# Rooms for the weight ring in two pools, a branch moved ahead of the last second products, and an inversion cut into five steps

## The chip, the cores and the metric

One core of a Trainium2 chip runs the kernel. The metric is the device time of one execution in microseconds, the median of several runs. Engines are called TensorE (PE in the rows), VectorE (DVE), ScalarE (ACT), GpSimd (POOL) and SyncE (SP); a "q" behind an engine's name means its queue of instructions (its sequencer).

## The reference, cut to what matters

256 tokens of width 1024 go through two layers, all in float32. The first is a hybrid of windowed attention and a gated delta rule; the second has two kinds of attention heads and then 32 experts, of which each token uses four, and a gated embedding at the end.

```python
def gated_deltanet(q, k, v, g, beta):            # chunks of 64 tokens
    m = where(strict, (k*beta) @ k.T * decay, 0)
    sol = triangular_solve(m + eye, concat([v*beta, k*beta*exp(G)]))   # unit lower triangle
    ...
def moe(u, ...):                                 # 256 tokens, top 4 of 32 experts
    hh = xs @ w_gu[e] + b_gu[e]                  # 1024 -> 2048 (first products)
    glu, lin = split(hh); glu = min(glu, 7); lin = clip(lin, -7, 7)
    act = glu * sigmoid(1.702*glu) * (lin + 1)
    return act @ w_dn[e] + b_dn[e]               # 1024 -> 1024 (second products)
def second_block(x, ...):
    ...
    h = h + moe(rmsnorm(h, g_moe), ...)
    u = rmsnorm(h, g_ple)
    h = h + sigmoid(u @ w_ple_gate) * (p @ w_ple_proj)
    return rmsnorm(h, g_final)
```

## The kernel before, in words

**Projections.** Weights of the dense layers come as pieces of 128 x 2048 float32 (1 MiB): `load` (L104) takes a room of a ring of rooms and issues the DMA on SP's queue, `piece` (L120) splits it with `split` (L314): ScalarE casts the high part, VectorE subtracts it from the source and leaves the low part. Each product is then three matmuls: activations' high part by the weights' high and low part, and activations' low part by the weights' high part. `proj_T_g` (L198) and `proj_tok_g` are generators that yield after a few products; `proj_rows` (L137) makes 256 rows by 1024 columns, 512 columns at a time, and hands each 128x512 result to a function that evacuates it.

**First stage.** `together` (L228) writes the program order: in each round every live generator (attention and delta rule, per half of the heads) makes one step, and then the fill (the projections) runs until its own count has reached 2.5 us. `gdn_half` (L597) is the delta rule for four heads. It writes its triangles to DRAM, reads them back as 64 blocks (`X`), inverts them on VectorE in `inverse` (L577: 15 columns, two operations for each), then pauses once, writes the blocks to `diag`, reads them back (L660), and transposes them on TensorE. The zeros of `diag` come from a tile that VectorE clears (L573). Within an engine's queue the tile framework's scheduler may order instructions otherwise than the program does, unless they are pinned with `keep_in_program_order`.

**The ring of weights.** SBUF pools are stacked. `st` lies low and has 3 rooms called raw, 2 whi and 2 wlo. After the first stage the pools `wa` (8 tiles of 4 KB per partition) and `wb` hold the second attention. When they close, the pool `raw2` (L1116) of 8 rooms (4 raw, 2 whi, 2 wlo; 64 KB per partition) takes their place: it covers `wa` (32 KB) and the first 32 KB of `wb`. The ring then has 15 rooms (`raws`, L1118). `ahead` (L1148) fills the first 11 of them, in the order of `raws` by program, before the experts start; `refill`, called after each product group in `run` (L1484), takes the room that was read. All weights of the 32 experts (384 MiB) go through it, raw, in 1 MiB loads.

**The experts.** `run` works through 17 units: pairs of experts, one expert of up to 128 rows, and the last expert, 31, alone. Step i does the first products of unit i, then the second products of unit i-1 (L1370 in both cases), `gated` (L1453: ScalarE and VectorE scale the result by the gates) and later `combine` (L1462: a matmul scatters it to tokens and VectorE adds to `hres`). Matmuls of `run` are pinned in program order.

**The tail.** After `run` the four loads of the gate weights (`gate_w`) go into the raw rooms of `raw2` and the first of them is split. `further` (L1618) is a branch on a register that counts tokens over the units' limits; with these inputs it is not taken. Then the last unit is combined, normed and transposed for both halves of the tokens (L1716 to L1729), with the splits of the other three gate pieces in between, the final projection runs on TensorE (`proj_rows` with four wide pieces) and `ev` (L1734) evacuates it: sigmoid, times the embedding, add, square for the final norm, and the output.

## Time and profile before

| what | value |
|---|---|
| median of 3 runs | 1570.43 us (1569.9 to 1571.59) |
| the profiled execution | 1570.8 us, its span 1568.9 us |
| busy share of the span | TensorE 91%, VectorE 39%, ScalarE 27%, GpSimd 2% |
| mean rate of the DMA over the span | 311 GB/s |
| operations on GpSimd | 39 |

The page cuts the span into 40 slices of 39.2 us. Up to slice 14 the core computes dense layers, from slice 15 to 38 the experts' weights stream in, and the last slice and a half hold the final projection. A timeline row gives the start, the busy time, the engine and line, the operation, how often it stands there in a row, and in brackets how long its engine was idle before it and who released it. Times that a row gives for a merged group run from its first start to its last end.

### The profile page before, as it was taken

To read this page: it belongs to the slowest core of one execution; us is meant where nothing else is said; L and a number is where in the kernel's file an instruction comes from. 1 tells how busy PE (TensorE), PEld (TensorE's weight loads), DVE (VectorE), ACT (ScalarE), POOL (GpSimd) and SP (SyncE) were. 2 spreads that over 40 slices of the span, in tenths; PEclk is the share of its full clock that TensorE was granted. 3 is DMA by queue.
4 is the path that set the end of the run, shared out by engine and by line. 5 is a ranking of instruction groups with operands and counts; after the bars stand their busy time and mean duration, and the time that the engine had idled before them with its cause. 6 is when DMAs were issued, how large, how long until landed. Compare 5 with 4: busy or idle time off the path is not lost. (4 is left out here: it accounts for less than half of the span.)

```text
span 1568.9 us, 20018 instructions
## 1 busy us (share of the span) xinstructions
PE 1431.5 (91%) x7922; PEld 883.2 (56%) x7922; DVE 619.3 (39%) x1215; ACT 418.6 (27%) x638; POOL 27.1 (2%) x39
## 2 busy tenths in 40 slices
PE   6999998999889989989888998999988889989887
PEld 6889898999689864424334334434433324424335
DVE  6868865456656662112123122112312202302236
ACT  5543644443447621101001001101100101101124
POOL 0000100000000000000000000000000000000000
PEclk9999999999899989999999999999999999999998
DMA  7544244355344189999999999999999999999981
GB/s 241 163 150 150 90 141 130 108 188 173 127 132 141 55 345 421 421 421 421 421 421 419 421 421 421 421 421 420 421 421 421 421 420 420 421 422 421 421 350 67
DMA packets 108541, 487.58 MB, mean 311 GB/s; under 512 B 14766, under 2 KB 23356, under 8 KB 59292
## 3 DMA queue, kind: packets, MB, share of 16 engines
q1 hardware_dynamic: 108300, 485.87, 78.2%
q8 instruction: 64, 1.05, 0.3%
q0 software_dynamic: 144, 0.39, 0.1%
q14 instruction: 33, 0.27, 0.0%
HBM read 483.48 MB, written 2.75 MB: 310 GB/s over the span
## 5 line engine op out<-in xcount | busy, mean ns | idle before, releaser
L1370 PE MATMUL ph<-raw,xs 128*64 128x512 f32 (+1 forms) x936 | 241.7, 594 | 5.7 <-DMA raw<-in_w_gu_dram 5.6
L1370 PE MATMUL ph<-wlo,xs 128*64 128x512 f32 (+1 forms) x552 | 192.3, 594 | 4.8 <-DMA wlo<-in_w_gu_dram 4.8
L1370 PE MATMUL ph<-whi,xs 128*64 128x512 f32 (+1 forms) x560 | 194.6, 594 | 2.0 <-DMA whi<-in_w_gu_dram 2.0
L316 DVE TENSOR_TENSOR wlo<-raw,whi 128x2048 fp32r<-128x2048 f32 (+4 forms) x73 | 158.0, 2165 | 91.8 <-ACT whi L315 91.7
L212 PE MATMUL pm<-w,wlo 128*128 128x256 f32 x640 | 182.5, 286 | 6.6 <-DVE wlo L316 6.6
L210 PE MATMUL pm<-w,whi 128*128 128x256 f32 x640 | 185.1, 290 | 3.3 <-ACT whi L315 3.3
L1557 DVE COPY hs<-ph 128x512 f32<-128x512 f32 x34 | 23.5, 692 | 406.4 <-PE ph L1370 406.4
L211 PE MATMUL pm<-w,whi 128*128 128x256 f32 x640 | 183.0, 286 | 0.0
L315 ACT CAST whi<-raw 128x2048 fp32r<-128x2048 f32 (+4 forms) x73 | 131.9, 1806 | 141.3 <-PE pm L211 88.1
L1370 PE MATMUL pm<-raw,act 128*64 128x512 f32 (+1 forms) x520 | 137.9, 597 | 29.0 <-DMA raw<-in_w_dn_dram 29.0
L1370 PEld LDWEIGHTS ph<-raw,xs 128*64 128x64 f32 (+1 forms) x936 | 78.1, 138 | 144.9 <-issue 130.8
L1557 ACT COPY hs<-ph 128x512 f32<-128x512 f32 x34 | 19.9, 586 | 412.6 <-PE ph L1370 412.6
L212 PEld LDWEIGHTS pm<-w,wlo 128*128 128x128 f32 x640 | 124.0, 194 | 7.5 <-DVE wlo L316 7.5
L210 PEld LDWEIGHTS pm<-w,whi 128*128 128x128 f32 x640 | 124.3, 194 | 4.1 <-ACT whi L315 3.9
L211 PEld LDWEIGHTS pm<-w,whi 128*128 128x128 f32 x640 | 124.5, 194 | 0.3
L1460 DVE SCALAR_TENSOR_TENSOR yl<-pm,gs,yh 128x512 fp32r<-128x512 f32 x32 | 24.0, 750 | 251.1 <-ACT yh L1459 250.4
L1370 PEld LDWEIGHTS ph<-wlo,xs 128*64 128x64 f32 (+1 forms) x552 | 61.6, 139 | 83.1 <-issue 72.8
L1370 PEld LDWEIGHTS ph<-whi,xs 128*64 128x64 f32 (+1 forms) x560 | 60.8, 138 | 81.5 <-issue 73.8
L1370 PEld LDWEIGHTS pm<-raw,act 128*64 128x64 f32 (+1 forms) x520 | 42.5, 137 | 113.6 <-issue 62.3
L1370 PE MATMUL pm<-wlo,act 128*64 128x512 f32 (+1 forms) x256 | 87.8, 597 | 11.8 <-DMA wlo<-in_w_dn_dram 11.5
L1459 ACT ACTIVATE yh<-pm,gs 128x512 fp32r<-128x512 f32 x32 | 22.0, 687 | 266.6 <-PE pm L1370 265.1
L1370 PE MATMUL pm<-whi,act 128*64 128x512 f32 (+1 forms) x248 | 82.5, 597 | 10.4 <-DMA whi<-in_w_dn_dram 10.4
(399 smaller groups left out, 1921.4 us busy)
## 6 DMA issues: line engine op xcount, KB each, us to landing
raw<-in_w_gu_dram SPq DMA_DIRECT2D x117, 1024.0 KB, 19.8
whi<-in_w_gu_dram SPq DMA_DIRECT2D x70, 1024.0 KB, 19.8
wlo<-in_w_gu_dram SPq DMA_DIRECT2D x69, 1024.0 KB, 19.8
raw<-in_w_dn_dram SPq DMA_DIRECT2D x65, 1024.0 KB, 19.8
raw<-in_w_in_dram SPq DMA_DIRECT2D x46, 1024.0 KB, 5.6
wlo<-in_w_dn_dram SPq DMA_DIRECT2D x32, 1024.0 KB, 20.0
whi<-in_w_dn_dram SPq DMA_DIRECT2D x31, 1024.0 KB, 19.8
raw<-in_w_branch_a_dram SPq DMA_DIRECT2D x4, 1024.0 KB
```

The costliest lines, as they stand in the source:

```text
L210: T.matmul(o, hi[:, k, ns], xh[:, k0 + k], start=first, stop=False)
L211: T.matmul(o, hi[:, k, ns], xl[:, k0 + k], start=False, stop=False)
L212: T.matmul(o, lo[:, k, ns], xh[:, k0 + k], start=False, stop=last)
L315: A.copy(hi, src)
L316: (by or V).tensor_tensor(lo, src, hi.bitcast(F32), ALU.subtract)
L1370: return tc.keep_in_program_order(T.matmul(*x_, **y_))
L1459: A.activation(yh[:, ns], yp[n_], AF.Copy, scale=b["gs"])
L1460: V.scalar_tensor_tensor(yl[:, ns], yp[n_], b["gs"], yh[:, ns].bitcast(F32), ALU.mult, ALU.subtract)
L1557: (V.tensor_copy if j // 2 else A.copy)(b["hs"][j // 2][:, j % 2 * 512:j % 2 * 512 + 512], hp[j])
```

## The change

1. *First products.* The load of the second half of x goes ahead of the two small vector loads on SP. The tile of zeros is cleared by GpSimd. `proj_T_g`, for a piece that was loaded ahead, does all products with the high part of the first piece first, and then those with the low part.
2. *Inversion.* `inverse` becomes a generator that pauses after every third column: five pauses, the last of which stands where the one pause behind it stood.
3. *Ring.* `raw2` keeps its 4 raw rooms; its whi and wlo rooms move to a pool of their own, `raw3`. The ring's order becomes raw2's raw, raw3's whi and wlo, then the rooms of `st`. The loads of `ahead` are pinned in program order on SP. Three tiles that nothing uses (640, 320 and 192 bytes per partition) shift the places of pools.
4. *Tail.* Every step of `run` ends with its outstanding combines. `further`, and behind it the four loads of the gate weights, is called in the last step ahead of the second products of the last unit. The gate pieces 1, 2 and 3 are all split behind the first half of the tokens, 2 and 3 with the subtraction on GpSimd. The last 128x512 group of the final projection is made and evacuated in two halves of 256 columns.

```diff
     SY.dma_start(ctab[0], a["const"][:, :cuts[1]])
+    SY.dma_start(hres[:, 1], xsrc[:, 1])
...
+    cst.tile([P, 160], F32, name="gap0")
...
-        SY.dma_start(raw[:, :kc * n].rearrange("p (k n) -> p k n", k=kc), src.rearrange(rows, p=P))
+        d_ = SY.dma_start(raw[:, :kc * n].rearrange("p (k n) -> p k n", k=kc), src.rearrange(rows, p=P))
+        if pin:
+            tc.keep_in_program_order(d_)
         return raw
...
             for nh in range(2):
+                for h in (0, 1) if halves and t and nh else (None,):
+                    ps = pp.tile([P, 512], F32, name=name)
+                    cs = slice(0, 512)
+                    if h is not None:
+                        ps, cs = ps[:, :256], slice(h * 256, h * 256 + 256)
...
+                    evac(t, nh, ps) if h is None else evac(t, nh, ps, h)
...
             hi, lo = piece(w[k0 * P:(k0 + 4) * P], 4, 512, raw and raw[k0 // 4])
+            if raw and k0 == 0:
+                for lo_ in range(2):
+                    for b in range(2):
+                        for j in range(2):
+                            ns = slice((2 * b + j) * P, (2 * b + j + 1) * P)
+                            o = ps[b][:, j * 256:(j + 1) * 256]
+                            for k in range(4):
+                                if lo_:
+                                    T.matmul(o, lo[:, k, ns], xh[:, k], start=False, stop=False)
+                                else:
+                                    T.matmul(o, hi[:, k, ns], xh[:, k], start=k == j == 0, stop=False)
+                                    T.matmul(o, hi[:, k, ns], xl[:, k], start=False, stop=False)
+                        yield 1.0 + lo_
+                continue
...
         SY.dma_start(v0[8 * i:8 * i + 8], a[n].rearrange("o (c p) -> (o c) p", p=P))
-    SY.dma_start(hres[:, 1], xsrc[:, 1])
...
-        V.memset(zero, 0.0)
+        G.memset(zero, 0.0)
...
                 V.tensor_tensor(o, o, tmp[:, :n, :m], ALU.subtract)
+                if j % 3 == 2:
+                    yield 0.0
...
-            inverse(X, Y)
-            yield 0.0
+            yield from inverse(X, Y)
...
     raw2 = ctx.enter_context(tc.tile_pool(name="raw2", bufs=1))
-    raws[:] = [(raw2, "raw", RAW2), (st, "raw", RAW), (raw2, "whi", 2), (raw2, "wlo", 2), (st, "whi", HL), (st, "wlo", HL)]
-    parts.append((raw2, 2))
+    raw3 = ctx.enter_context(tc.tile_pool(name="raw3", bufs=1))
+    raws[:] = [(raw2, "raw", RAW2), (raw3, "whi", 2), (raw3, "wlo", 2), (st, "raw", RAW), (st, "whi", HL), (st, "wlo", HL)]
+    parts.append((raw3, 2))
...
-        return [(load(src, kc, m, pool, rows), kc, m) for src, kc, m, rows in (next(order) for _ in range(n))]
+        return [(load(src, kc, m, pool, rows, True), kc, m) for src, kc, m, rows in (next(order) for _ in range(n))]
...
+                if i == n and ahead_of_last:
+                    ahead_of_last()
                 if i:
                     b = units[i - 1]
...
-                if i != n - 1:
-                    flush()
+                flush()
                 after(i)
...
             every = raws[:]
-            raws[:] = [(st, "raw", RAW)]
+            raws[:] = [(st, "whi", HL)]
...
             raws[:] = every
+            gate_w.extend(rows_piece(a["w_ple_gate_2"][0], i, big) for i in range(4))
...
-        last = run(units, order, ready, {-1: first, 2: [load_biases], ...})
+        last = run(units, order, ready, {-1: first, 2: [load_biases], ...}, None, further)
...
         count[1] = 0
-        gate_w = [rows_piece(a["w_ple_gate_2"][0], i, big) for i in range(4)]
         gate_w[0] = piece(None, 4, 512, gate_w[0])
-
-        further()
-        count[1] = 1
...
-            for i in ((1, 2), (3,))[t]:
-                gate_w[i] = piece(None, 4, 512, gate_w[i])
+            if t == 0:
+                gate_w[1:] = [piece(None, 4, 512, g_, by) for g_, by in zip(gate_w[1:], (V, G, G))]
...
-        proj_rows(ph, None, None, xh, xl, ev, gate_w, 4, "ph")
+        proj_rows(ph, None, None, xh, xl, ev, gate_w, 4, "ph", True)
```

Left out are the argument lists, the two other unused tiles, and `ev` and `total`, which take the half `h` and add three sums of squares in place of two.

## Rows read from the trace of the kernel before

**Rows 1.** The page: GB/s moved in each of 40 equal slices of 39.2 us.
```profile
GB/s 241 163 150 150 90 141 130 108 188 173 127 132 141 55 345 421 421 421 421 421 421 419 421 421 421 421 421 420 421 421 421 421 420 420 421 422 421 421 350 67
```

**Rows 2.** Windows: length, busy us of PE, PEld, DVE, ACT, POOL, clock, DMA, GB/s.
```profile
0.00:440.00 440.00, 407.92 (x2903) 381.61 (x2904) 290.08 (x488) 211.22 (x287) 18.16 (x24) 0.98 0.46 148
...
558.00:1522.00 964.00, 879.62 (x4167) 378.15 (x4167) 224.80 (x555) 113.66 (x187) 3.02 (x5) 0.99 1.01 420
```

**Rows 3.** Timeline of TensorE, 0 to 20 us: start, busy, operation, idle before, releaser.
```profile
13.82 0.58 PE L210 MATMUL pm<-w,whi 128*128 128x256 f32 x1 [2.38 <-ACT whi L315]
...
16.45 0.58 PE L212 MATMUL pm<-w,wlo 128*128 128x256 f32 x1 [1.41 <-DVE wlo L316]
```

**Rows 4.** Timeline of TensorE around 126 and 247 us.
```profile
125.94 0.38 PE L212 MATMUL pm<-w,wlo 128*128 128x256 f32 x1 [2.51 <-DVE wlo L316]
...
247.16 1.94 PE L304 MATMUL pm<-C,w 128*128 128x128 f32 x8 [4.79 <-DMA w<-diag]
```

**Rows 5.** Windows at the first inversion and behind the gap after it.
```profile
111.20:123.50 12.30, 12.23 (x102) 12.03 (x101) 11.81 (x44) 5.51 (x5) 0.00 (x0) 1.00 0.53 171
128.00:132.00 4.00, 4.00 (x25) 4.00 (x25) 2.36 (x8) 0.59 (x1) 0.00 (x0) 0.66 1.07 358
```

**Rows 6.** Lines L736 and L795: duration ns min/median/max, first and last start, form.
```profile
L736 ACT ACTIVATE w<-pm,gdnw x4: 678/680/682, 190.2 to 311.3; 128x512 f32<-128x512 f32 x4
...
L795 ACT ACTIVATE w<-pm x8: 582/597/606, 270.5 to 346.2; 128x512 f32<-128x512 f32 x8
```

**Rows 7.** Timeline of SP, 470 to 600 us: DMA issues.
```profile
531.13 27.90 SPq L116 DMA_DIRECT2D raw<-in_w_gu_dram  x7
...
585.51 10.63 SPq L116 DMA_DIRECT2D raw<-in_w_gu_dram  x7
```

**Rows 8.** One window ahead of the stream.
```profile
522.00:557.00 35.00, 32.38 (x181) 26.80 (x180) 19.83 (x31) 15.21 (x24) 2.20 (x4) 0.95 0.16 61
```

**Rows 9.** Timelines of TensorE and VectorE between 514 and 600 us.
```profile
521.35 0.66 PE L304 MATMUL pm<-C,w 128*128 128x128 f32 x4 [0.94 <-ACT w L386]
...
556.29 0.68 DVE L316 TENSOR_TENSOR w<-w,w 128x512 fp32r<-128x512 f32 x1
...
581.83 10.94 PE L1370 MATMUL ph<-raw,xs 128*64 128x512 f32 x49
```

**Rows 10.** Timeline of TensorE at 1471 us and in the tail.
```profile
1471.19 3.65 PE L1370 MATMUL pm<-raw,act 128*64 128x512 f32 x14 [1.32 <-DMA raw<-in_w_dn_dram]
...
1521.64 1.94 PE L1370 MATMUL pm<-wlo,act 128*64 128x512 f32 x8 [0.28 <-SPq L1623]
1523.51 2.24 PE L1370 MATMUL pm<-hs,ohT 128*128 128x512 f32 x8
1529.82 0.47 PE L1370 MATMUL pm<-yh,ohT 128*128 128x512 f32 x1 [4.07 <-DVEq L1623]
...
1537.91 0.50 PE L159 MATMUL ph<-wlo,raw 128*128 128x512 f32 x1 [1.19 <-DVE wlo L316]
```

**Rows 11.** Line L1623, the branch: sequencers' durations ns, first and last start.
```profile
L1623 SPq EVENT_SEMAPHORE  x9: 17/17/17, 1518.4 to 1530.0; - x9
...
L1623 PEldq COMPARE_BRANCH  x1: 3822/3822/3822, 1525.0 to 1525.0; - x1
L1623 ACTq COMPARE_BRANCH  x1: 50/50/50, 1525.7 to 1525.7; - x1
```

**Rows 12.** Timelines of SP and VectorE in the tail.
```profile
1509.37 21.14 SPq L116 DMA_DIRECT2D raw<-in_w_ple_gate_dram  x4
...
1516.18 1.57 DVE L1460 SCALAR_TENSOR_TENSOR hs<-pm,gs,hs 128x512 fp32r<-128x512 f32 x2 [11.75 <-ACT hs L1459]
...
1527.33 2.29 DVE L316 TENSOR_TENSOR wlo<-raw,whi 128x2048 fp32r<-128x2048 f32 x1
```

**Rows 13.** Groups of GpSimd: xcount, busy us, mean ns, idle before.
```profile
L299 POOL TENSOR_TENSOR l_r<-rs_t,C 128x4 f32<-128x4 f32 x12 | 14.0, 1167 | 281.6 <-DVE rs_t L298 281.6
```

**Rows 14.** Timeline of ScalarE behind the last product.
```profile
1560.65 0.69 ACT L1738 ACTIVATE sw<-ph,n_r 128x512 f32<-128x512 f32 x1 [2.54 <-PE ph L160]
```

More of the change, by code (lines that the diff above doesn't have):

```diff
@@ L102, in slots, with load @@
         return sum(n_ for _, _, n_ in raws)
-    def load(src, kc, n, pool=None, rows="(k p) n -> p k n"):
+    def load(src, kc, n, pool=None, rows="(k p) n -> p k n", pin=False):
         if pool is None:
@@ L135, in rows_piece, with proj_rows @@
         return load(W[k0 * P:(k0 + 4) * P, nh * 512:(nh + 1) * 512], 4, 512, pool)
-    def proj_rows(pp, w, W, xh, xl, evac, raw=(), wide=2, name="pm"):
+    def proj_rows(pp, w, W, xh, xl, evac, raw=(), wide=2, name="pm", halves=False):
         pcs = []
@@ L398, in rope @@
         V.tensor_tensor(dst, t1, t2, ALU.add)
+    sm.tile([P, 80], F32, name="gap1", bufs=1)
     keep = Pool(ctx.enter_context(tc.tile_pool(name="keep", bufs=1)), w4=4)
@@ L407, in tile_net @@
         both = ctx.enter_context(tc.tile_pool(name="both", bufs=1))
+        both.tile([P, 48], F32, name="gap2")
         pm = c1.enter_context(tc.tile_pool(name="ps", bufs=4, space=bass.MemoryType.PSUM))
@@ L1482, in bias_of, with run @@
             return bi
-        def run(units, order, ready, more=None, room=None):
+        def run(units, order, ready, more=None, room=None, ahead_of_last=None):
             more = more or {}
@@ L1655, in further @@
             raws[:] = every
+            gate_w.extend(rows_piece(a["w_ple_gate_2"][0], i, big) for i in range(4))
         big = raw2, RAW2
-        pv, emb = [], []
+        pv, emb, gate_w = [], [], []
         def load_embed(nxt):
@@ L1687, in tile_net @@
         first = [lambda nxt, g=g: g() for g in (chosen, gates, changes, overflow)]
-        last = run(units, order, ready, {-1: first, 2: [load_biases], 3: [biases], 4: [blocks], 6: [load_embed], EMB - 1: [embed]})
+        last = run(units, order, ready, {-1: first, 2: [load_biases], 3: [biases], 4: [blocks], 6: [load_embed], EMB - 1: [embed]}, None, further)
         if "h3" in dbg:
@@ L1706, in tile_net, with total @@
         rr = []
-        def total(t):
+        def total(t, n=2):
             s1 = sm.tile([P, 1], F32, name="po_s1")
-            V.tensor_tensor(s1, ssq[:, t, 0:1], ssq[:, t, 1:2], ALU.add)
+            if n == 2:
+                V.tensor_tensor(s1, ssq[:, t, 0:1], ssq[:, t, 1:2], ALU.add)
+            else:
+                V.tensor_reduce(s1, ssq[:, t], AX.X, ALU.add)
             return rsqrt(s1, 1, 1.0 / D, EPS, "n_r")
@@ L1727, in tile_net, with ev @@
             rr.append(total(t))
-            for i in ((1, 2), (3,))[t]:
-                gate_w[i] = piece(None, 4, 512, gate_w[i])
-        ssq = sm.tile([P, 2, 2], F32, name="po_ss")
+            if t == 0:
+                gate_w[1:] = [piece(None, 4, 512, g_, by) for g_, by in zip(gate_w[1:], (V, G, G))]
+        ssq = sm.tile([P, 2, 3], F32, name="po_s3", bufs=1)
         og = {}
-        def ev(t, nh, ps):
-            ns = slice(nh * 512, nh * 512 + 512)
+        def ev(t, nh, ps, h=None):
+            cs = slice(0, 512) if h is None else slice(h * 256, h * 256 + 256)
+            ns = slice(nh * 512 + cs.start, nh * 512 + cs.stop)
             o = hres[:, t, ns]
-            sg = wk.tile([P, 512], F32, name="sw", bufs=4)
+            sg = wk.tile([P, 512], F32, name="sw", bufs=4)[:, cs]
             A.activation(sg, ps, AF.Sigmoid, scale=rr[t][:, :1])
@@ L1740, in ev @@
             V.tensor_tensor(o, o, sg, ALU.add)
-            A.activation(sg, o, AF.Square, accum_out=ssq[:, t, nh:nh + 1])
-            og[nh] = wk.tile([P, D], F32, name="hs", bufs=2)[:, :512]
-            V.tensor_tensor(og[nh], o, gf[:, ns], ALU.mult)
-            if nh == 0:
+            i = nh + (h or 0)
+            A.activation(sg, o, AF.Square, accum_out=ssq[:, t, i:i + 1])
+            if not h:
+                og[nh] = wk.tile([P, D], F32, name="hs", bufs=2)[:, :512]
+            V.tensor_tensor(og[nh][:, cs], o, gf[:, ns], ALU.mult)
+            if nh == 0 or h == 0:
                 return
-            r = total(t)
+            r = total(t, 2 + t)
             for b in range(2):
```

12 lines of the change are left out of this document (5 added, 7 removed).

## The prediction, on record before the change was run

> **What bounds the kernel now.** I read the slices of the page first, then the windows by stage, then the timelines around each place that the change touches. There are four stages. Up to about 440 us (the hybrid layer) TensorE is the bound: it is busy 407.9 of 440 us [rows 2], so whatever takes away idle time of TensorE there comes off the total. From 440 to 558 us the second attention block runs; the weight transfers have almost stopped (55 GB/s in slice 14, [rows 1]). From 558 to 1522 us the experts' weights stream in at 421 GB/s in nearly every slice [rows 1], while TensorE has idle time, 879.6 busy of 964 us [rows 2]: here the stream is the bound, one load of 1 MiB costs 1.0486 MB / 421 GB/s = 2.49 us, and only an earlier start (or a higher rate) helps. The last gap of TensorE that a weight load ends is at 1471 us [rows 10]; behind it the tail is a chain of TensorE, the branch and the last projection. So savings before the stream and in the tail add up, as long as the stream's rooms stay full.
>
> The trace is one execution of 1570.8 us (span 1568.9 and 1.9 around it); the median shown is 1570.43. I make the sum against the profiled run and take it off the median: the two differ by 0.4 us.
>
> **Part 1, the first products.** The first projection product waited 2.38 us for a cast that stands behind both halves of the first norm, and the first product with a low part waited 1.41 us for VectorE [rows 3]. The load of the second half of x goes ahead of the two small vector loads on SP's queue (these come later by one 512 KB load), the memset leaves VectorE, and the high products go first: 2 groups of 4 x 4 x 2 = 32 products at 0.12 us (102 products in 12.23 us, [rows 5]) are 3.8 us of cover for a low part that came 2.6 us after the first product (16.45 - 13.82). So the 1.41 goes wholly; of the 2.38 I take 0.6, since only one of its causes moves. Sum -2.0; bounds 0 (the small vectors, now later, hold the first evacuation) and -3.8. The memset of 128x512 goes to GpSimd, which has nothing else to do there; the two DMAs that read it come a little later and their readers only with the first inversion.
>
> **Part 2, the inversion in five steps.** No operation is added or taken away; the one pause behind it becomes five (after columns 2, 5, 8, 11 and 14, the last where the old one stood). So each chain gets four more rounds of at least 2.5 us of projection work by the planner's count, in program order. In the first inversion VectorE was busy 11.81 of 12.3 us [rows 5] and the low part of the next weight piece stood behind it: TensorE lost 2.51 us at 125.94 [rows 4], and its granted clock was 0.66 in the four microseconds from 128 (the lower of 1.2 and 2.4 GHz for part of it), another 0.34 x 4 = 1.4 us [rows 5]. With pieces between the steps the low part comes first: -3.9. In the second inversion VectorE had time, and the gap of 4.79 us at 247.16 waits for the trip through memory behind it [rows 4]; a loss of clock follows as behind the first. Four rounds give 10 us more cover; the chain itself becomes longer by the VectorE work of that fill (two splits of 2.29 us, [rows 12], and evacuations, some 5 to 7 us by that row). I take half of 4.79, -2.4, and count no clock. Of the -6.3 I give back 0.8 for waits that appear elsewhere: -5.5. Bounds: -10.1 (both gaps and twice the clock) and +4.8 (one more gap like the largest one). The later end is covered: the last evacuation of the two chains stands at 311.3, the last of the fill at 346.2 [rows 6], 35 us for 10 us of delay.
>
> **Part 3, the start of the ring.** Seven first loads go out from 531.13 [rows 7], but from 522 to 557 only 61 GB/s moved, 2.1 MB or two loads [rows 8]: the scheduler put rooms of `st` first, and the room `raw2` covers the attention pools `wa` and `wb` and so waits for the last work in `wb`, VectorE's 128x512 subtraction at 556.29 [rows 9]. `raw2` is now half as large and lies on `wa` alone, whose last reader is TensorE's transposes at 521.35 to 522.0 [rows 9]. Its four loads, pinned in order, can go at 522; then SP stands waiting at the first room of `raw3` until 556.9, and behind it are queued the three `st` rooms that went early before, which cost two loads of the old order. Nothing else waits on SP there: the next loads need rooms anyway. Four loads instead of two before 557 are 2 x 2.49 = 5.0 us. What is late next: there are 15 rooms, so 11 loads remain, 11 x 2.49 = 27.4 us from 557, done at 584.4 (the delay from issue to first byte stands at both ends and cancels), and the first room comes free for a refill at 585.51 [rows 7], which follows the first products at 581.83 [rows 9] that no load sets. The stream pauses for 1.1 us at this rate, for less where the loads come slower; I take 0.8: -4.2, bounds -2.7 (a pause of 2.3, when the second refill is late too) and -5.0.
>
> **Part 4, the tail.** Before: second products of the last unit to 1523.6, combine of the pair before it, branch, combine of the last at 1529.82 after 4.07 us of idle [rows 10]; SP stood inside the branch until its third gate load had landed at 1530.0, so the fourth left only then [rows 11, 12]. After: second products of the last pair end at about 1516.1 as now, when VectorE begins to gate them [rows 12]; its combine must wait for its gated rows (VectorE ends at 1517.75) and takes 2.24 us [rows 10], to 1520.0. Then the branch. Its compare-and-branch took 3.82 us on TensorE's sequencer, 0.05 us on ScalarE's [rows 11]. TensorE reached it 0.74 us before the end of the combine (1525.01 against 1525.75), so the last unit's products start between 1520.1 and 1523.2; I take the TensorE row, 1523.2. They take 7.4 us, 1.4 us more if the idle time lowers the clock as behind the gaps above: 1532.0, and gating 2 us: 1534.0, against 1529.8. Given back: between combine and projection VectorE did a split of 2.29 us [rows 12], which now follows; the continuous part of the projection started at 1537.9 to 1538.5 [rows 10] and now starts at about 1540, 1.7 later. The gate loads leave together when SP is out of the branch (1521.6, the landing of the last weight piece, [rows 10]), and cannot all be in before 1521.6 + 4 x 2.49 = 1531.6; the last is needed some 8 us into the projection. The last group is split into halves: the chain behind the last product has four operations of 0.69 us [rows 14], now of half width, -1.1 by estimate (0 to -1.4), and 48 products of 0.12 for 24 of 0.227 cost +0.3. Tail: +1.7 + 0.3 - 1.1 = +0.9, taken as +1.0; bounds -2 (short branch, full clock) and +6.
>
> Two of the gate splits go to GpSimd, whose only operation in the trace is a power of 128x4 in 1.17 us [rows 13]. Bounds for 128x2048: 2.29 us as on VectorE [rows 12], and 512 times 1.17, absurdly far; I take the first, since it is the same operation. With casts done by about 1534 and 1536.5 and the last low part needed at 1540 + 36 x 0.227 = 1548.2, two operations one after the other cost nothing up to T = 7 us each. The Trainium skill speaks against the move: "GPSIMD Engine Reference", section 3.1, gives 4497 ns for this operation against 2293 ns on VectorE, and calls VectorE the rule for elementwise work. VectorE's row agrees (2.29 us); GpSimd's figure no trace here shows yet; taken alone the rule says that the move loses 4.4 us of engine time, and by the point just worked out none of the kernel's.
>
> **Sum.** -2.0 - 5.5 - 4.2 + 1.0 = -10.7: 1570.4 - 10.7 = 1559.7, say 1560.
>
> **Rivals.**
> *The lead is not there* (the change doesn't do what it says): `raw2` still waits for `wb`. Then nothing is loaded by 557, the `st` rooms being pinned behind, and part 3 is +5.0 in place of -4.2: 1569. For it: before, one room waited for two pools. Against it: 64 KB became 32, as large as `wa`. Chance 0.10.
> *Covered elsewhere*: parts 1 and 2 only move idle time (the next cast or split is late instead), part 3 and the tail stay: 1570.4 - 4.2 + 1.0 - 0.7 = 1566.5. For it: VectorE at 11.81 of 12.3 us has no room to give. Chance 0.12.
> *Slower: GpSimd is late.* The last pieces' low parts run one after the other on GpSimd, and TensorE waits for the second: 2 x (T - 7) us. From T = 7 it costs, from T = 14 the whole is slower than before by over 0.2%; at T = 15 it is 1576. For it: 1.17 us for four columns. Against it: that is a power, not a subtraction. With what the branch may add at its upper bound it decides earlier, from T = 11.5. Chance 0.12.
> *A faster stream.* The unused tiles shift every room by 640, 960 or 1152 bytes. If the transfers' rate hangs on where a room starts, a gain of, say, 1.5% over 385 loads of 2.49 us (959 us) would be 14.5 us more: 1545. TensorE could follow (879.6 of 964, [rows 2]). Against it: the rate is 421 in almost every slice, though they differ in which rooms they fill [rows 1]. Chance 0.06. The Trainium skill ("DMA: Bandwidth & Descriptors", section "How a descriptor splits into AXI transactions") has such a rule: a descriptor that doesn't start on 256 bytes takes an extra transaction; the trace of before can't show it, as all rooms of the stream stand alike.
>
> **How the numbers follow.** The forecast has 0.60 and by its own bounds reaches from 1552 to 1568. Up to 1570 it takes in "covered elsewhere" and "the lead is not there"; the faster stream and the slow GpSimd stay outside, 0.18. A measurement here tells 0.2%, 3.1 us. Faster: 0.60 + 0.12 + 0.06 = 0.78; within: 0.10; slower: 0.12.
>
> **What would show it.** Right: no gap at TensorE by 16, 126 and a shorter one by 247; four weight loads by 525 and the next at 547 to 549 (all earlier by parts 1 and 2); a stream that begins some 9 us earlier in all and a last weight landing at about 1510; TensorE's branch of 3.8 us ahead of the last products; GpSimd with two operations of 2 to 7 us. Wrong: four first loads that wait for VectorE; a new gap in 100 to 320; a rate other than 421; a gap in the last projection that GpSimd ends.

## The result, and the profile after

| | before | after |
|---|---|---|
| median, in one session on one chip | 1570.74 us (4 runs, 1569.9 to 1571.59) | 1553.56 us (4 runs, 1548.98 to 1557.41) |
| ratio | | 0.9886, 95% interval 0.9871 to 0.9901 |
| two later sessions, ratio | | 0.9896 (0.9882 to 0.9911) and 0.9875 (0.9857 to 0.9892) |
| the profiled execution | 1570.8, span 1568.9 | 1549.0, span 1547.2 |

The change makes the kernel 17 us faster. The forecast was 1560; the time lies within the range and near its lower end, and not for the reasons given: of the forecast's four parts the first showed no gain and the second brought less than half of its term, and two effects of where buffers start in memory, one of them held for unlikely and one not thought of, brought more than half of the gain.

The page of after, the clock and the rate by slices (38.7 us each), which answers [rows 1]:

```profile
PEclk9999999999999999999999999999999999999999
...
GB/s 247 164 152 159 109 104 145 132 169 188 115 147 133 132 340 424 424 424 425 424 423 422 424 424 424 425 424 424 424 424 424 425 423 424 424 425 424 424 325 88
```

422 to 425 GB/s stand where 419 to 422 stood, in every slice of the stream. Then the start of the ring, first SP's queue and then two windows (length, busy us by engine, clock, DMA share, GB/s), which answer [rows 7] and [rows 8]:

```profile
513.23 2.09 SPq L118 DMA_DIRECT2D raw<-in_w_gu_dram  x4
547.16 0.80 SPq L118 DMA_DIRECT2D whi<-in_w_gu_dram  x2
...
549.27 1.45 SPq L118 DMA_DIRECT2D raw<-in_w_gu_dram  x3
...
574.34 4.36 SPq L118 DMA_DIRECT2D raw<-in_w_gu_dram  x4
```

```profile
513.00:547.00 34.00, 31.23 (x182) 25.86 (x181) 19.91 (x32) 15.22 (x24) 2.19 (x4) 1.00 0.31 124
557.00:575.00 18.00, 15.04 (x90) 11.88 (x91) 14.65 (x95) 3.52 (x8) 1.72 (x3) 0.81 1.01 414
```

Four loads go out at 513.2, and all four have come when the pool `wb` is done; 124 GB/s over 34 us are 4.2 MB, the four of them, where before it were two; the other rooms follow from 547.2, and the first refill leaves at 574.3 while the queue is still full (414 GB/s up to 575, no pause). TensorE up to the first products, the rows that answer [rows 3], [rows 4] and [rows 9]:

```profile
5.98 0.25 PE L327 MATMUL pm<-C,vrow 16*128 16x16 f32 x1 [5.98 <-DMA vrow<-in_g_moe_dram]
...
15.20 0.38 PE L222 MATMUL pm<-w,whi 128*128 128x256 f32 x1 [2.79 <-ACT whi L338]
...
122.56 0.39 PE L233 MATMUL pm<-w,whi 128*128 128x256 f32 x1 [1.45 <-ACT whi L338]
...
124.94 0.58 PE L235 MATMUL pm<-w,wlo 128*128 128x256 f32 x1 [1.65 <-DVE wlo L339]
...
205.46 1.06 PE L327 MATMUL pm<-C,w 128*128 128x128 f32 x8 [1.76 <-DVE w L758]
...
212.75 1.94 PE L327 MATMUL pm<-C,w 128*128 128x128 f32 x16 [0.81 <-DVE w L758]
...
565.35 5.38 PE L1396 MATMUL pm<-dd,w 128*128 128x128 f32 x32 [1.11 <-DVE dd L1409]
570.66 7.09 PE L1396 MATMUL ph<-raw,xs 128*64 128x512 f32 x32
```

The first projection product starts at 15.20, later than before (13.82), and the wait of 1.41 behind it is gone. The gap of 4.79 at 247 is gone; 1.76 and 0.81 stand at 205 and 213, and at 122 to 125 1.45 and 1.65 stand where 2.51 stood. The clock behind that place fell as it did before, here of before and of after:

```profile
124.00:132.00 8.00, 6.06 (x38) 6.06 (x39) 6.36 (x11) 1.36 (x2) 0.00 (x0) 0.79 0.72 205
...
124.00:132.00 8.00, 7.06 (x47) 7.06 (x48) 6.23 (x15) 0.75 (x2) 0.00 (x0) 0.79 0.73 244
```

The granted clock was 0.79 both times, part of the stretch at 1.2 of 2.4 GHz, while from 240 to 252 us it is now 1.00 (0.79 from 244 to 252 before). The tail, TensorE, the branch, GpSimd and VectorE in turn ([rows 10] to [rows 13]):

```profile
1495.19 2.23 PE L1396 MATMUL pm<-hs,ohT 128*128 128x512 f32 x7 [0.29 <-DVE hs L1486]
1498.88 3.65 PE L1396 MATMUL pm<-wlo,act 128*64 128x512 f32 x16 [1.46 <-DVEq L1649]
...
1505.90 0.50 PE L1396 MATMUL pm<-yh,ohT 128*128 128x512 f32 x1
...
1511.77 0.50 PE L167 MATMUL ph<-wlo,raw 128*128 128x512 f32 x1 [1.05 <-DVE wlo L339]
...
1520.30 0.50 PE L167 MATMUL ph<-wlo,raw 128*128 128x512 f32 x1 [0.83 <-POOL wlo L339]
...
1525.87 0.50 PE L167 MATMUL ph<-wlo,raw 128*128 128x512 f32 x1 [2.50 <-POOL wlo L339]
```

```profile
L1649 SPq EVENT_SEMAPHORE  x9: 17/17/17, 1480.6 to 1500.5; - x9
...
L1649 PEldq COMPARE_BRANCH  x1: 363/363/363, 1496.0 to 1496.0; - x1
...
L1649 DVEq EVENT_SEMAPHORE  x1: 21/21/21, 1498.8 to 1498.8; - x1
```

and VectorE's semaphore in the branch of before:

```profile
L1623 DVEq EVENT_SEMAPHORE  x1: 21/21/21, 1529.7 to 1529.7; - x1
```

```profile
1515.61 4.63 POOL L339 TENSOR_TENSOR wlo<-raw,whi 128x2048 fp32r<-128x2048 f32 x1 [688.08 <-ACT whi L338]
...
1521.20 4.61 POOL L339 TENSOR_TENSOR wlo<-raw,whi 128x2048 fp32r<-128x2048 f32 x1
```

```profile
1521.33 4.51 DVE L1734 TENSOR_TENSOR po_s<-po_ss 128x1 f32<-128x1 f32 x1
1525.87 0.15 DVE L321 TENSOR_SCALAR rs_t<-po_s 128x1 f32<-128x1 f32 x1
```

The branch takes TensorE's sequencer 0.36 us and not 3.82; the last unit's products start 1.46 us behind the combine. In both kernels TensorE goes on 0.1 to 0.2 us behind VectorE's semaphore in the branch. Before, VectorE had its split of 2.29 us ahead of that semaphore (1527.33 to 1529.62, [rows 12]), which came 0.8 us behind the end of TensorE's own branch (1528.83); now only the last addition of a combine stands there, and the split comes later. GpSimd's subtraction takes 4.6 us, and the last projection waits for it twice, 0.83 and 2.50 us. From the landing of the last weight piece (1521.6 before, at 1500.3 now, by SP's last waits in the branch) to the end of the span it is 47.3 us before and 46.9 after.

### The profile page after: what moved, and what is told of

Its sections match the earlier page's. It is cut to its first block, busy times and chain, and to the rows that moved or that the text cites. A ratio compares the mean times of both kernels' runs of the same rounds, so it can differ in the third digit from the quotient of the medians.

```text
span 1547.2 us, 20071 instructions
## 1 busy us (share of the span) xinstructions
PE 1419.1 (92%) x7946; PEld 873.2 (56%) x7946; DVE 619.7 (40%) x1215; ACT 419.0 (27%) x641; POOL 36.1 (2%) x42
## 5 line engine op out<-in xcount | busy, mean ns | idle before, releaser
L1396 PE MATMUL ph<-raw,xs 128*64 128x512 f32 (+1 forms) x960 | 281.3, 594 | 2.2 <-DMA raw<-in_w_gu_dram 2.2
L1396 PE MATMUL ph<-whi,xs 128*64 128x512 f32 (+1 forms) x552 | 187.5, 594 | 4.3 <-DMA whi<-in_w_gu_dram 4.3
L1396 PE MATMUL ph<-wlo,xs 128*64 128x512 f32 (+1 forms) x536 | 177.9, 593 | 3.0 <-DMA wlo<-in_w_gu_dram 3.0
L233 PE MATMUL pm<-w,whi 128*128 128x256 f32 x624 | 177.7, 285 | 2.3 <-ACT whi L338 2.3
L235 PE MATMUL pm<-w,wlo 128*128 128x256 f32 x624 | 174.3, 281 | 4.2 <-DVE wlo L339 4.2
L234 PE MATMUL pm<-w,whi 128*128 128x256 f32 x624 | 175.0, 281 | 0.1
L1396 PEld LDWEIGHTS ph<-raw,xs 128*64 128x64 f32 (+1 forms) x960 | 92.0, 139 | 136.6 <-issue 125.5
L235 PEld LDWEIGHTS pm<-w,wlo 128*128 128x128 f32 x624 | 117.6, 189 | 4.8 <-DVE wlo L339 4.8
L233 PEld LDWEIGHTS pm<-w,whi 128*128 128x128 f32 x624 | 118.0, 189 | 3.0 <-ACT whi L338 2.8
L234 PEld LDWEIGHTS pm<-w,whi 128*128 128x128 f32 x624 | 118.1, 189 | 0.6 <-DVE w L339 0.5
L1396 PE MATMUL pm<-wlo,act 128*64 128x512 f32 (+1 forms) x272 | 95.4, 597 | 13.1 <-DMA wlo<-in_w_dn_dram 11.7
L1396 PE MATMUL pm<-whi,act 128*64 128x512 f32 (+1 forms) x264 | 89.9, 597 | 10.3 <-DMA whi<-in_w_dn_dram 10.3
```

Of the source, the lines that this page charges most:

```text
L233: T.matmul(o, hi[:, k, ns], xh[:, k0 + k], start=first, stop=False)
L234: T.matmul(o, hi[:, k, ns], xl[:, k0 + k], start=False, stop=False)
L235: T.matmul(o, lo[:, k, ns], xh[:, k0 + k], start=False, stop=last)
L1396: return tc.keep_in_program_order(T.matmul(*x_, **y_))
```

## The experiments

Every session timed the kernel before beside the others: 1571.57 us in the first (e1 to e4), 1571.90 in the second (e5 to e8), 1572.37 in the third (e9 to e12). Ratios are to the kernel before of the same session, with 95% intervals; medians are compared with those of the same session where there is one, and with the mean ratio of the changed kernel, 0.9886, otherwise.

### e1 and e12: the changed kernel again

No edit.

> The changed kernel once more, unaltered. Theory (rooms): of its 15 rooms the 7 of st start on a multiple of 256 bytes, the 8 of raw2 and raw3 32 bytes past one; packets of 8192 bytes take 309 ns into the first and 314 to 315 ns into the second, so the stream runs at 424 GB/s in every run, and the spread of the first four times (1549 to 1557) has another cause, in TensorE's granted clock: times at 1549 to 1557 again, and a profile with 424 in the slices of the stream whatever its clock. Rival (chance): 424 GB/s belonged to the fastest run alone, which was the one profiled; a profile of a slower run shows 421.

> The changed kernel once more, beside the two runs above on the same chip: 1553 to 1557, and a first product of the experts between 1 and 5 us earlier or later than in the two other profiles of it, by how many stretches at the lower clock its first 570 us hold.

Measured: 1555.52 us (0.9896) and 1551.10 (0.9875). The stream ran at 424 GB/s in both profiles, so the rate does not belong to one lucky run. The spread has another cause: of TensorE's clock, the window 440 to 460 us of the profiles of after and of e1:

```profile
440.00:460.00 20.00, 19.70 (x144) 19.10 (x145) 12.52 (x33) 10.26 (x20) 1.10 (x2) 1.00 0.48 144
...
440.00:460.00 20.00, 18.85 (x122) 18.53 (x122) 12.02 (x32) 8.23 (x14) 1.10 (x2) 0.83 0.34 95
```

The same kernel ran this stretch once at the upper level throughout and once with part of it at the lower of 1.2 and 2.4 GHz (0.83), which cost 0.17 x 20 = 3.4 us; in both it followed the same short waits of TensorE between 430 and 441 us (1.76, 0.86 and 1.59 us). What decides between the two is open. It means that single profiles of these kernels can differ by some 3 us up to the stream, and that a part of the change worth 1 or 2 us must be judged by timed medians and not by two profiles. e12's median came out below its expectation, and so did its profile: the window at 1.00, the first product of the experts at 570.61, as in after (570.66) and 5.1 us ahead of e1 (575.75). From there to the end the three profiles differ less: 976.5 us in after and e12, 978.4 in e1.

### e2, e3 and e4: where the rooms start

The changed kernel without the three unused tiles (e2); with the third one larger (e3); the kernel before with one unused tile and nothing else (e4).

```diff
# e2: after, minus
-    cst.tile([P, 160], F32, name="gap0")
-    sm.tile([P, 80], F32, name="gap1", bufs=1)
-        both.tile([P, 48], F32, name="gap2")
# e3: after, with
-        both.tile([P, 48], F32, name="gap2")
+        both.tile([P, 104], F32, name="gap2")
# e4: before, plus
+    cst.tile([P, 32], F32, name="gap0")
     RAW, HL = 3, 2
```

> The changed kernel without its three unused tiles; st starts 128 bytes past a multiple of 256 as in the kernel before, raw2 and raw3 160 bytes past one. Theory (rooms): all packets take 314 ns, the stream is back at 421 GB/s, and the time is 0.7% of 960 us = 6.8 us above the changed kernel's. Rival (order and pools): the rate came with the new order of rooms, the pinned loads or the two pools; 424 GB/s stays and the time is that of the changed kernel within 1 us.

> The changed kernel with the third unused tile at 416 bytes in place of 192, which moves raw2 and raw3 by 224 bytes to a multiple of 256; now all 15 rooms start on one. Theory (rooms): every packet takes 309 ns, 428 GB/s, 959 us x 8/15 x 1.6% = 8 us below the changed kernel's time, some 1545 us. Rival (order and pools): no change within 1 us.

> The kernel before with one unused tile of 128 bytes ahead of the pool st, nothing else; all 15 rooms then start on a multiple of 256 bytes. Theory (rooms): packets of 309 ns for 314, 428 GB/s for 421, 959 us x 1.6% = 15 us faster than before: 1555. If TensorE or the order of refills binds before that, less, but over 8 us. Rival (order and pools): 421 GB/s and 1570.

Measured: e2 1562.33 us (0.9943, 0.9930 to 0.9955), e3 1550.34 (0.9864, 0.9849 to 0.9878), e4 1557.58 (0.9915, 0.9902 to 0.9928). The rates by slice of e2, e3 and e4:

```profile
GB/s 245 162 151 161 104 114 133 136 163 202 98 140 134 135 332 422 420 422 421 421 420 420 421 421 422 421 422 421 421 421 421 421 420 421 421 421 421 422 326 77
...
GB/s 246 163 152 155 113 98 151 121 170 172 138 113 163 136 281 409 427 426 427 427 427 425 427 427 426 427 426 427 426 427 426 427 426 427 427 427 426 427 347 65
...
GB/s 246 163 151 151 89 145 129 110 172 181 139 113 162 55 313 426 427 427 426 427 427 425 427 427 427 427 426 427 427 426 427 427 427 426 427 427 426 428 352 67
```

421, 427 and 427 GB/s. The landings of the loads say the same room by room. Mean us from the landing of one load to that of the next, by the room of the later one, for the 15 rooms in the ring's order (some 20 rounds in the middle of the stream, without the loads that were over 0.3 us off 2.47):

```
before  2.49 2.49 2.49 2.49 2.48 2.49 2.49 2.48 2.48 2.48 2.49 2.49 2.48 2.48 2.49   all rooms 128 bytes past a multiple of 256
after   2.49 2.49 2.51 2.50 2.50 2.50 2.49 2.48 2.44 2.44 2.43 2.45 2.45 2.43 2.45   first 8 rooms 32 bytes past one, last 7 rooms on one
e3      2.45 2.46 2.43 2.44 2.45 2.46 2.45 2.44 2.46 2.45 2.45 2.46 2.48 2.44 2.44   all rooms on one
```

A packet of 8192 bytes took 314.0 ns in the mean of the stream's middle in before, 311.1 in after and 309.5 in e3. The packets' times do not tell the rooms of after apart as sharply as the expectation of e1 has it: the first three of the eight slow rooms still show 309 to 311 ns, the following ones up to 315. Why is open.

So one tile of 128 bytes that nothing uses makes the old kernel 14.0 us faster, and without its unused tiles the change is worth 9.2 us (1562.33 against 1571.57) and not 16. The rival "order and pools" falls. Nor do all of these 9.2 us belong to the schedule: in e2 the working pools still start where e9 below puts them. e2 and e9 have every room and every working pool at the same place, and differ in the change itself: 0.9943 against 0.9975, 5.0 us (2.5 to 7.5 by the two intervals), are what its four parts bring together. e3 fell short: 5.2 us below the changed kernel by the medians (2 to 8 by the intervals of the ratios) and not 8. Its slice 16 moved 409 GB/s, about 1.6 us lost (18/427 of 38.8). A window of its profile shows where, in the rate at the end of the row and the DMA's share before it:

```profile
580.00:585.00 5.00, 5.00 (x26) 1.64 (x24) 3.23 (x23) 0.12 (x1) 0.00 (x0) 1.00 0.79 306
585.00:590.00 5.00, 5.00 (x26) 1.72 (x24) 0.00 (x0) 0.00 (x0) 0.00 (x0) 1.00 0.99 405
```

Here the rooms do run out: the first products began at 579.4 and the first refill left at 583.1. And e3's first part was slower, which led to e9: its first product of the experts starts 3.7 us later than e1's (579.43 against 575.75), and from there to the end it takes 971.0 us against 978.4.

### e5: the inversion in one piece

```diff
-                if j % 3 == 2:
-                    yield 0.0
-            yield from inverse(X, Y)
+            inverse(X, Y)
+            yield 0.0
```

> The changed kernel with the inversion as before, in one piece with one pause. Theory (cover): the gap of 4.8 us at TensorE behind the second inversion and its low clock come back, and the gap at 126 us grows by up to 1 us: 5 to 7 us slower than the changed kernel. Rival (covered elsewhere): other waits take the gap's place, within 1.5 us of the changed kernel.

Measured: 1556.30 us, 0.9902 (0.9887 to 0.9917); by the mean ratio of the changed kernel 2.5 us slower than it, by its own interval 0 to 5 (the changed kernel's uncertainty comes on top, so that no effect is not excluded). The gap comes back, as TensorE's row shows:

```profile
244.65 1.94 PE L327 MATMUL pm<-C,w 128*128 128x128 f32 x8 [4.93 <-DMA w<-diag]
```

It lies between the two expectations and nearer to the rival: the largest gap of 4.9 us and the low clock behind it are what the pauses take away, but the waits at 205, 213 and 124 us come in their place (1.76 + 0.81, of which e5 has neither, and 1.45 + 1.65 for 2.69). From the transposition at 75 us to the one at 418 us the profile of after needs 343.2 us (74.89 to 418.08), that of e5 344.8 (74.94 to 419.77). The pair e2 and e9 differs by 2.6 us in the same stretch (344.1 against 346.7).

### e6: the ring alone

```diff
# before, with
+    raw3 = ctx.enter_context(tc.tile_pool(name="raw3", bufs=1))
+    raws[:] = [(raw2, "raw", RAW2), (raw3, "whi", 2), (raw3, "wlo", 2), (st, "raw", RAW), (st, "whi", HL), (st, "wlo", HL)]
+    parts.append((raw3, 2))
# and the loads of ahead pinned in program order
```

> The kernel before with the rooms in two pools, the new order of the ring and the pinned loads, and nothing else; no room moves in memory. Theory (lead): four loads before VectorE's last use of the second pool in place of two, 2 x 2.49 = 5.0 us less, and up to 0.8 lost again when the rooms run out: 4.2 to 5.0 us faster than before, at 421 GB/s. Rival (rooms run out): the stream pauses ahead of the first refill and no more than 2.5 us stay.

Measured: 1567.28 us, 0.9968 (0.9956 to 0.9980): 4.6 us by the medians, 5.0 by the ratio. SP's first loads:

```profile
520.96 2.13 SPq L116 DMA_DIRECT2D raw<-in_w_gu_dram  x4
```

All four leave at 521 to 523, as soon as TensorE's last transposes out of `wa` are through (520.27 to 520.93). The lead is there, and hardly any of it is lost again.

### e7: the branch where it was

```diff
# after, with further, the gate loads, the first gate split and the last combine of a pair behind run again
-                flush()
+                if i != n - 1:
+                    flush()
-        last = run(units, order, ready, {...}, None, further)
+        last = run(units, order, ready, {...})
```

> The changed kernel with the branch, the gate loads, the first gate split and the last combine of a pair where they were before, behind the last unit's second products; the two splits on GpSimd and the halves stay. As the prediction had it (the branch costs 3.8 us of TensorE in either place and moves onto its path): 1 to 2 us faster than the changed kernel. Rival, from the trace of the changed kernel (the branch took 0.36 us there, and the projection began 9.9 us behind the last weight's landing in place of 14.1): 2 to 4 us slower.

Measured: 1557.25 us, 0.9906 (0.9890 to 0.9921), some 3 us slower than the changed kernel by the mean ratio, with intervals that touch. The branch, TensorE, GpSimd and VectorE:

```profile
L1650 PEldq COMPARE_BRANCH  x1: 3578/3578/3578, 1506.6 to 1506.6; - x1
```

```profile
1511.42 0.77 PE L1396 MATMUL pm<-yh,ohT 128*128 128x512 f32 x1 [4.07 <-DVEq L1650]
...
1521.86 0.79 PE L166 MATMUL ph<-whi,raw 128*128 128x512 f32 x1 [5.05 <-ACT raw L338]
```

```profile
1513.89 4.51 POOL L339 TENSOR_TENSOR wlo<-raw,whi 128x2048 fp32r<-128x2048 f32 x1 [682.79 <-ACT whi L338]
```

```profile
1514.11 6.45 DVE L339 TENSOR_TENSOR wlo<-raw,whi 128x2048 fp32r<-128x2048 f32 x1
```

The branch behind the last products is again 3.58 us long, and the 4.07 us of idle time are back; VectorE's semaphore stands at 1511.3, behind its split of the first gate piece (1508.93 to 1511.21). The other traces agree on the place: 3.44 to 4.18 us in the five with the branch behind the last products (before, e4, e6, e7, e9), 0.36 in the nine with it ahead. But this run does not price the branch alone: GpSimd's first subtraction now falls on VectorE's own split, which takes 6.45 us in place of 2.28, and the projection starts 5.05 us late for that. The sign is the rival's (the branch ahead is the better place); the size stays mixed with GpSimd's.

### e8: all later gate splits on VectorE

```diff
-                gate_w[1:] = [piece(None, 4, 512, g_, by) for g_, by in zip(gate_w[1:], (V, G, G))]
+                gate_w[1:] = [piece(None, 4, 512, g_, by) for g_, by in zip(gate_w[1:], (V, V, V))]
```

> The changed kernel with all three later gate splits on VectorE. Theory (GpSimd late): its two subtractions take 4.6 us each, and the last projection waited 0.8 and 2.5 us for them; on VectorE they take 2.3 each, so 2.5 to 3.3 us faster than the changed kernel. Rival (VectorE full): the second half of the tokens is then late by as much, within 1 us of the changed kernel or slower. As the prediction had it (no cost up to 7 us each): within 1 us.

Measured: 1548.87 us, 0.9847 (0.9834 to 0.9861): 6.1 us faster than the changed kernel by the mean ratio, 3 to 9 by the two intervals. TensorE's waits of the tail:

```profile
1501.20 3.65 PE L1396 MATMUL pm<-wlo,act 128*64 128x512 f32 x16 [1.46 <-DVEq L1649]
...
1514.55 0.50 PE L167 MATMUL ph<-wlo,raw 128*128 128x512 f32 x1 [1.30 <-DVE wlo L339]
```

No wait behind the first low part is left; 3.3 us of waits for GpSimd are gone, as the theory had it. The rest of the difference lies in the spread of e1 and e12: from the first product of the experts to the end the profile of e8 takes 972.9 us, 3.6 less than those of after and e12. The prediction's claim that GpSimd costs nothing falls.

### e9: where the working pools start

```diff
# before, plus
+    sm.tile([P, 8], F32, name="gap1", bufs=1)
     keep = Pool(ctx.enter_context(tc.tile_pool(name="keep", bufs=1)), w4=4)
```

> The kernel before with one unused tile of 32 bytes in the pool sm; the rooms of st stay where they were, the working pools of the first two stages (which hold the activations' high and low parts) start 32 bytes past a multiple of 64 in place of on one, and raw2 160 past one of 256 in place of 128. Theory (moving operand): in the changed kernel most of the 256-column products of the first stage follow each other in 0.116 us, in the kernel before in 0.120, and the experiments so far split along this start modulo 64 alone; so 0.116 here too, the first stage 4 to 5 us shorter at 421 GB/s: 1566 to 1567.5. Rival (weights or pools): the faster pitch comes from where st stands, or from another part of the change; 0.120 and 1571.

Measured: 1567.89 us, 0.9975 (0.9965 to 0.9985), 4.5 us faster, at 421 GB/s. The window 312 to 342 us, which holds little but 256-column products and no idle time, of before, after, e3 and e9; the number to read is the first in brackets, TensorE's matmuls in 30 us at the full clock:

```profile
312.00:342.00 30.00, 30.00 (x252) 30.00 (x252) 16.53 (x11) 12.48 (x11) 0.00 (x0) 1.00 0.53 176
...
312.00:342.00 30.00, 30.00 (x258) 29.83 (x257) 18.29 (x12) 15.86 (x15) 0.90 (x1) 1.00 0.53 176
...
312.00:342.00 30.00, 30.00 (x252) 29.91 (x251) 17.43 (x13) 15.66 (x15) 1.44 (x2) 1.00 0.46 150
...
312.00:342.00 30.00, 30.00 (x260) 30.00 (x259) 17.04 (x12) 14.00 (x12) 0.00 (x0) 1.00 0.53 176
```

252 in before and e3, whose working pool starts on a multiple of 64 bytes (128 and 0 past one of 256); 258 and 260 in after and e9, where it starts 32 bytes past one. That is 0.119 us a product against 0.116. The rooms of `st` with the other operand stand 128 past a multiple of 256 in before and e9, on one in after and e3, so they don't set the pitch. The same window splits all fourteen traces: 257 to 260 products in the ten whose pool starts 32 bytes past a multiple of 64, 252 or 253 in the four where it starts on one (before, e3, e4, e6). With 1920 such products the difference is worth some 5 us by estimate, part of which e3, on a multiple of 64, gave back of what the rooms brought. In the changed kernel the 32 bytes are an accident of part 4: the three sums of squares need a tile of 24 bytes (`po_s3` in pool `sm`), which takes 32; the three unused tiles are 1152 bytes together, a multiple of 64.

### e10: both starts, and the splits on VectorE

```diff
# after, with
+        both.tile([P, 104], F32, name="gap2")           # in place of 48: all 15 rooms on a multiple of 256
+        wk.tile([P, 8], F32, name="gapw")               # first tile of wk
+        wa.tile([P, 8], F32, name="gapa")               # first tile of wa
+                gate_w[1:] = [piece(None, 4, 512, g_, by) for g_, by in zip(gate_w[1:], (V, V, V))]
```

> The changed kernel with all 15 rooms on multiples of 256 bytes, the working pools of the first two stages moved 32 bytes past them by a tile of 32 bytes inside those pools, and the later gate splits on VectorE. Theory (both starts): 427 GB/s as with all rooms aligned, 0.116 us for the products, no wait for GpSimd: 8 us below the run with the splits on VectorE and some 5 us of it against the aligned run by the products: 1540 to 1542. Rival: the two starts exclude each other, 1547 to 1549.

Measured: 1543.14 us, 0.9816 (0.9803 to 0.9829), the fastest of all, 29 us below the kernel before. The page's rates, and the window of e9:

```profile
GB/s 247 164 152 153 94 114 159 110 165 190 140 100 178 137 259 426 426 427 427 426 427 425 427 427 426 427 426 426 427 427 426 427 426 426 427 427 426 426 338 123
```

```profile
312.00:342.00 30.00, 30.00 (x258) 29.82 (x257) 18.20 (x16) 15.84 (x15) 2.02 (x2) 1.00 0.48 155
```

426 to 427 GB/s and 258 products: the two starts do not exclude each other. The time missed the expectation by 1 to 3 us: 4.9 us below e8 by the ratios and not 8, 7.5 below e3 with the 3.3 us for GpSimd in it. Its first product of the experts stands only 2.7 us ahead of e3's (576.70 against 579.43); why not 5 was not found.

### e11: the first products as before

```diff
# after, with the loads of x and of the vectors in the old order, V.memset, and
-            if raw and k0 == 0:
+            if False:
```

> The changed kernel with its first part undone: the loads of x and of the vectors in the old order, the memset on VectorE, and the low products among the high ones. As the prediction had it: 2 us slower than the changed kernel. Rival, from the traces of the changed kernel (the first projection product starts 1.2 to 1.5 us later than before, because a transposition of the two vectors stands ahead in TensorE's queue and their loads now come later; the 1.4 us behind it are gone): within 0.5 us.

Measured: 1554.32 us, 0.9885 (0.9870 to 0.9900), the changed kernel's own mean ratio; 3.2 us above e12 and 1.7 below what e1's ratio gives beside this run's own kernel before (0.9896 x 1572.4 = 1556.0). No effect can be told from none. TensorE's first rows:

```profile
14.80 0.58 PE L232 MATMUL pm<-w,whi 128*128 128x256 f32 x1 [2.38 <-ACT whi L337]
...
17.43 0.58 PE L234 MATMUL pm<-w,wlo 128*128 128x256 f32 x1 [1.41 <-DVE wlo L338]
```

The wait of 1.41 is back behind the first product, and the first product is 0.4 earlier than in after. (In this execution the second half of x came 1 us later than in the profile of before, so two profiles can't settle what is left.)

## Why the prediction was right and where it was wrong

Sign and range held; the sum of -10.7 stood against -17.2. That the time lies where it does is luck: the four parts that the sum was made of bring 5.0 us together (e2 against e9), about half of what was forecast, and two effects outside the sum bring 11. Term by term:

**Part 1, -2.0: did not show.** The 1.41 us went, as predicted. The step that failed is the one taken on the load of x. It came no earlier (ScalarE starts on the second half at 6.67, before at 6.66), and the bound named for the loss ("the small vectors, now later, hold the first evacuation") was what happened, one step earlier: the transposition of the vectors stands at the head of TensorE's queue, at 5.98 in after for 4.67 before, and the transposes behind it came later (8.75 for 6.84). The first product starts 1.4 us later and the two cancel. e11 finds no effect, with an uncertainty of 2 us.

**Part 2, -5.5: mis-sized.** The mechanism was right for the second inversion: the gap of 4.79 us and the low clock behind it are gone, and e5 brings the gap back. It was sized at -2.4, half of the gap and no clock; two waits of 1.76 and 0.81 us came in its place. What failed is the first inversion's -3.9, "with pieces between the steps the low part comes first": at 122.56 a product with the high part waits 1.45 us for ScalarE, at 124.94 the one with the low part still waits 1.65 us for VectorE, 3.1 us together for 2.51 before, and the clock falls as before (0.79). VectorE was busy from 120 to 125 us without a break, as "covered elsewhere" had it, so that rival holds half of the truth. e5 gives 2.5 us for the five steps, with an interval from 0 to 5.

**Part 3, -4.2: right.** 4.6 to 5.0 us in e6. The pause was set at 0.8 and is next to nothing: the first refill left 3.7 us behind the first product both times (585.51 - 581.83 before, 574.34 - 570.66 after), and the queue still held loads then. Of the profiles shown only e3's, with a faster stream and a late first product, ran into it.

**Part 4, +1.0: the sum nearly right, its steps wrong.** 47.3 us from the last landing to the end became 46.9 in the profile of after. That is luck: two errors nearly cancelled. The 3.82 us of TensorE's branch were priced as if they moved with the branch; they did not (0.36). The last thing that TensorE waited for was VectorE's semaphore in the branch, which came behind a split before and comes without it now; so the last products started 1.46 us behind the combine, no clock was lost on them (1.00 from 1498 to 1506), and the continuous part of the projection began at 1511.77, 11.5 us behind the last landing, where the prediction had 18.4 (1540 - 1521.6). And because it began so early, GpSimd was late: the point T = 7 had been worked out from a projection that starts at the later time. With the measured 4.6 us for each, one behind the other from 1515.61 to 1525.81 with a small power of the first norm between them, the projection waited 3.3 us for them. The bound from VectorE's row (2.29) was off by a factor of two; the Trainium skill's figure of "GPSIMD Engine Reference", section 3.1, 4497 ns, agrees with the measured 4.6 us, and its rule (elementwise work on VectorE) is borne out by e8.

**The faster stream, held for unlikely (0.06): came, for the half of the rooms.** The price of 14.5 for all rooms was right (e4: 14.0); the change moves only the 7 rooms of `st` onto a multiple of 256 bytes (by 640; the 8 others move by 1184 and not by 1152, the tile of part 4 included), and e1 against e2 gives 6.8. The step that failed is the evidence set against it. "421 in almost every slice, though they differ in which rooms they fill" says nothing, since all rooms stood 128 bytes past a multiple of 256, as the last sentence of the same paragraph said itself. The Trainium skill's rule in "DMA: Bandwidth & Descriptors", section "How a descriptor splits into AXI transactions", speaks of what a transaction reads: a descriptor that starts off a multiple of 256 bytes begins at the boundary below, and the bytes that are not used cost beats. What was moved here is the start in the destination. In sign the runs agree: 2.49 us a load off a multiple, 2.44 to 2.45 on one in the mean. In size they don't: counted in the page's beats of 32 bytes a start 32 bytes off would cost a quarter of one 128 bytes off, and both cost the same.

**The pitch of the products, not foreseen.** e9: 4.5 us by the medians, 2.4 to 5.5 by the ratio, from 32 bytes.

With rate 6.8, ring 4.6, pitch 4.5, inversion 2.5 and the rest at zero the sum is 18.4, against 16 to 21 us in the three sessions. So of the forecast's own four parts 5 to 7 us came (5.0 by e2 against e9, 7.1 by e5 and e6), and 11 came from where things start in memory; each of these numbers is uncertain by 2 to 3 us.

## What to carry to other kernels

Before anything is said of a streaming kernel's rate, look at where its rooms start: a few unused bytes ahead of a pool can be worth more than a rearranged schedule, and a change that only shifts addresses has to be undone by itself before its gain is put down to what it meant to do. An observation that can't come out otherwise (all rooms alike) is no evidence against a rival. When work goes to an idle but slower engine, work out its due time from the earliest start that the rest of the change allows, and count which operations of the other engine it holds up.

## What the runs showed of the hardware that was not expected

- Where the destination of a load starts changes its rate: 1 MiB lands every 2.44 to 2.45 us in the mean in rooms on a multiple of 256 bytes (some 427 GB/s when all are, e3, e4 and e10) and every 2.49 in rooms 32, 128 or 160 bytes past one (421 GB/s; before, e2 and e9), in after side by side, 7 rooms on a multiple and 8 that start 32 bytes past one.
- Products of 256 columns follow each other in 0.116 us when the pool that holds the moving operand starts 32 bytes past a multiple of 64, and in 0.119 when it starts on one. Which of the operands in that pool does it was not taken apart.
- A VectorE operation with two inputs in SBUF can stand still for as long as GpSimd's lasts: a sum of two 128x1 columns took 4.51 us beside GpSimd's 4.61 (0.15 otherwise), a split 6.45 us (2.28 otherwise); in the same stretches operations with an input in PSUM ran at their usual 0.68. A sum of two columns that starts together with GpSimd's first subtraction (1515.63 against 1515.61) still took 0.15. The Trainium skill says in "GPSIMD Engine Reference", section 1, that GpSimd shares its SBUF interfaces with VectorE and contends with instructions that have two SBUF inputs; the rows agree, and here the wait lasted until the other instruction was done.
- The branch that is not taken took TensorE's sequencer 3.44 to 4.18 us behind the last products (five traces) and 0.36 us ahead of them (nine traces), in before and after alike behind the products of a combine. Why was not found.
